# Hybrid encoder layer on one core: the SSD's skip weights in one load of 64-byte rows, sorted by head on GpSimd

## Chip, cores and metric

The kernel runs on one core of a Trainium2 chip. Its time is the time of one execution on the device in microseconds (us); lower is better. A profiled execution gives the rows that are read here. Its span runs from the first to the last instruction.

## The reference, cut to what matters

The program computes one layer of a streaming encoder over 256 tokens of width 1024, in float32: a layer norm, one wide input projection, three mixers (Mamba-2 SSD, RWKV-7, HGRN2), their gated sum, an output projection, a second layer norm, and a mixture of 16 experts with a last layer norm. The part that the change touches is the skip term of the SSD: each of its 16 heads has one weight, `d_skip`, by which the head's input is added to its output.

```
y = y_diag + y_off + xs * d_skip.astype(f32).reshape(SSD_GROUPS, hg)[:, :, None]
```

The RWKV-7 mixer stands beside it in time. Per chunk of 64 tokens it needs the inverse of a triangular matrix for each head, which the kernel gets by forward substitution.

## The kernel before

Activations stand with features on the 128 partitions and tokens along the row. `stream()` (lines 331 to 371) is the inner work of every projection: weights come from memory in pieces of 512 KB into `raw` (line 339, on SyncE's queue, SP), ScalarE (ACT) rounds them to `whi` (line 183), VectorE (DVE) takes the rest `wlo` (line 184), and TensorE (PE) does three products for each tile (lines 366 to 368). There are four buffers of each kind, so a late `wlo` stops TensorE as soon as what is ready is used up.

`mixers()` sets the order. Two halves of the RWKV heads are prepared by `rwkv_part()`, in two calls each. Behind the third call stands the first solve, `rwkv_solve(0)`: GpSimd (POOL) has written the score blocks to DRAM (`ed`, line 536), SyncE's queue loads them again with one system of equations to a partition (`eu`, line 582, four loads of 128 KB in rows of 128 bytes; in the profile both ends are named, as arena<-ed), and VectorE scales them (lines 588, 589) and runs 32 steps of substitution (lines 593, 595). Then comes `ssd_dt_start()`, which issues the loads of the SSD's small vectors on GpSimd's queue behind the last write of `gd` (line 451), and then the fourth `rwkv_part()`. The second solve follows later, from 175 us.

In `ssd_dt_start()` the tile `hp` takes `ssd_dt_bias` and `ssd_a_log` (line 942), each broadcast to 128 partitions as rows of 16 floats, 64 bytes. The tile `dsk` takes the skip weights (line 944) in the order in which the SSD uses them: partitions 0 to 63 hold the even heads, partitions 64 to 127 the odd ones, 8 floats to a partition. The source steps by two floats, so every float is a piece of 4 bytes. `dsk` is read from 449.7 us on (line 1079).

The order of the instructions on each engine is worked out when the program is built, by a planner that goes through the program with its own costs and priorities. Each engine then runs its own list in that order and waits where an operand is not there.

Of the kernel before, what the change touches and what calls it, by code (L numbers as in the profile page):

```python
# [7 lines left out]
F32 = mybir.dt.float32  # L8
# [79 lines left out]
def dram(t, offset, ap):  # L88
    return bass.AP(tensor=t.tensor, offset=t.offset + offset, ap=ap)
# [50 lines left out]
class Kern:  # L140
# [794 lines left out]
    def ssd_dt_start(self):  # L935

        nc, A = self.nc, self.A
        hp = self.hp16 = self.c1.tile([128, 2, 16], F32, name="hp16")
        self.dsk = self.c1.tile([128, 8], F32, name="dsk")
        with self.tc.issue_after(self.later_dma.ins):  # L940
            for i, nm in enumerate(("ssd_dt_bias", "ssd_a_log")):
                nc.gpsimd.dma_start(hp[:, i, :], dram(A[nm], 0, [[0, 128], [1, 16]]))
            for h in range(2):
                nc.gpsimd.dma_start(self.dsk[h * 64:h * 64 + 64, :], dram(A["ssd_d"], h, [[0, 64], [2, 8]]))
        self.sdt = self.c1.tile([128, 5, 16], F32, name="sdT")
        ex = self.dtx = self.c1.tile([128, 2, 16], F32, name="dtx")
        dt = self.sdt[:, 0:2, :]
        ps = self.feat(COL_DT, ncol=16)[:16, 0, :]
        xr = self.rwt.tile([128, L], F32, name="sq")[:16]
        nc.scalar.activation(xr, ps, AF.Copy)  # L950
        ps = self.pmm.tile([128, 2, 16], F32, name="mm")
        for t in range(2):
            nc.tensor.transpose(ps[:, t, :], xr[:, t * 128:(t + 1) * 128], self.ident[:16, :16])
        nc.vector.tensor_tensor(dt, ps, hp[:, 0:1, :].to_broadcast([128, 2, 16]), op=OP.add)
        nc.vector.scalar_tensor_tensor(ex, dt, -1.0, dt, op0=OP.mult, op1=OP.min)
        nc.scalar.activation(hp[:, 1, :], hp[:, 1, :], AF.Exp)
        return nc.scalar.activation(ex, ex, AF.Exp)
# [773 lines left out]
```

## Time and profile before

| | us |
|---|---|
| three runs, median (lowest to highest) | 830.51 (830.09 to 830.99) |
| the profiled execution, its own time | 829.69 |
| its span, first to last instruction | 827.9 |
| TensorE busy in it | 784.8 (95%) |
| VectorE busy in it | 510.1 (62%) |

The profiled execution is 0.82 us under the median; 1.79 us of its time lie outside the span. An engine's busy share is a mean over all stages, so the rows of a stage count for a change in that stage.

### The profile page before, as it was taken

The page shows a single profiled execution, that of the slowest core. Times are in us where ns is not written, and L with a number is a line of the kernel's source. Part 1 is how long each engine was busy: PE and PEld are TensorE (multiplying, and loading weights), DVE is VectorE, ACT ScalarE, POOL GpSimd, SP SyncE. Part 2 cuts the span into 40 slices and gives each one's busy share as a digit, 9 for nine tenths or more (in the row PEclk, how much of TensorE's full clock was granted, in tenths as well). Part 3 has the DMA queues.
Part 4 walks back from the last instruction along what each step waited for, and adds up shares of the span by engine and source line. Part 5 has one row for each costly group of instructions (what it writes and reads, how often), then busy time and mean ns, then how long its engine had stood idle before and what let it go on. Part 6 is the DMA issues. An engine that isn't in the chain of part 4 may idle for free. (4 is left out here: it accounts for less than half of the span.)

```text
span 827.9 us, 16484 instructions
## 1 busy us (share of the span) xinstructions
PE 784.8 (95%) x6354; PEld 604.5 (73%) x6354; DVE 510.1 (62%) x1150; ACT 369.7 (45%) x824; POOL 134.7 (16%) x204
## 2 busy tenths in 40 slices
PE   7999969999999999999998999999999999999991
PEld 5898859988898899898797999999444434443440
DVE  6897669999997555567579887785611111111136
ACT  3755445574645555645477755453412121211111
POOL 3364614450102001102002111000000000001201
PEclk9999969999999999999899999999999999999996
DMA  7544564575445455366179568985999999999941
GB/s 229 177 118 114 50 161 119 140 180 155 107 132 148 128 155 153 103 203 193 38 237 299 178 205 283 349 271 161 390 386 386 387 387 386 387 386 386 386 179 54
DMA packets 146526, 183.93 MB, mean 222 GB/s; under 512 B 25609, under 2 KB 94472, under 8 KB 146440
## 3 DMA queue, kind: packets, MB, share of 16 engines
q1 hardware_dynamic: 142888, 176.91, 65.3%
q0 software_dynamic: 1504, 3.20, 2.2%
q10 hardware_dynamic: 2048, 2.70, 1.0%
q8 instruction: 52, 0.85, 0.4%
q14 instruction: 34, 0.28, 0.1%
HBM read 180.12 MB, written 2.65 MB: 221 GB/s over the span
## 5 line engine op out<-in xcount | busy, mean ns | idle before, releaser
L183 ACT ACTIVATE whi<-raw 128x512 fp32r<-128x512 f32 x268 | 165.5, 623 | 162.9 <-PE st L367 126.3
L184 DVE TENSOR_TENSOR wlo<-raw,whi 128x512 fp32r<-128x512 f32 x268 | 189.1, 715 | 77.3 <-ACT whi L183 64.2
L368 PE MATMUL st<-hhi,wlo 128*128 128x256 f32 (+1 forms) x744 | 212.0, 293 | 9.0 <-DVE wlo L184 8.8
L366 PE MATMUL st<-hhi,whi 128*128 128x256 f32 (+1 forms) x744 | 210.0, 290 | 2.2 <-ACT arena L784 1.4
L367 PE MATMUL st<-hlo,whi 128*128 128x256 f32 (+1 forms) x744 | 208.4, 288 | 0.0
L368 PEld LDWEIGHTS st<-hhi,wlo 128*128 128x128 f32 (+1 forms) x744 | 140.3, 192 | 16.6 <-DVE wlo L184 10.8
L366 PEld LDWEIGHTS st<-hhi,whi 128*128 128x128 f32 (+1 forms) x744 | 140.5, 192 | 7.1 <-issue 2.6
L367 PEld LDWEIGHTS st<-hlo,whi 128*128 128x128 f32 (+1 forms) x744 | 140.3, 192 | 3.1 <-issue 1.6
L1445 PE MATMUL b<-arena,xg 128*64 128x512 f32 x288 | 78.8, 596 | 0.0
L367 PE MATMUL st<-ylo,whi 128*128 128x256 f32 x192 | 53.8, 288 | 1.5 <-DVE ylo L184 1.5
L366 PE MATMUL st<-yhi,whi 128*128 128x256 f32 x192 | 53.9, 287 | 0.0
L368 PE MATMUL st<-yhi,wlo 128*128 128x256 f32 x192 | 53.1, 287 | 0.4 <-DVE wlo L184 0.2
L1445 PEld LDWEIGHTS b<-arena,xg 128*64 128x64 f32 x288 | 23.9, 137 | 38.0 <-issue 34.5
L1515 DVE SCALAR_TENSOR_TENSOR elo<-b,egs,ehi 128x512 fp32r<-128x512 f32 x15 | 11.3, 750 | 60.7 <-ACT ehi L1514 60.7
L1495 PE MATMUL b<-arena,ehT 128*64 128x512 f32 x144 | 43.0, 596 | 0.0
L367 PEld LDWEIGHTS st<-ylo,whi 128*128 128x128 f32 x192 | 36.4, 192 | 2.1 <-DVE ylo L184 1.7
L368 PEld LDWEIGHTS st<-yhi,wlo 128*128 128x128 f32 x192 | 36.2, 193 | 1.0 <-DVE wlo L184 0.8
L366 PEld LDWEIGHTS st<-yhi,whi 128*128 128x128 f32 x192 | 36.5, 192 | 0.3 <-ACT yhi L183 0.2
L1360 POOL TENSOR_TENSOR arena<-arena 128x512 f32<-128x512 bf16 x4 | 4.5, 1158 | 197.2 <-PE b L1445 197.2
L1484 ACT ACTIVATE ehT<-b 128x256 f32<-128x256 f32 x16 | 6.2, 389 | 67.7 <-PE b L1483 67.7
L1476 DVE SCALAR_TENSOR_TENSOR ehi<-ehi,b 128x256 f32<-128x256 f32 x16 | 6.0, 418 | 47.2 <-PE b L1445 47.2
L593 DVE TENSOR_TENSOR arena<-arena 128x1 f32<-128x1 f32 (+15 forms) x64 | 34.0, 531 | 0.8
(448 smaller groups left out, 1431.0 us busy)
## 6 DMA issues: line engine op xcount, KB each, us to landing
raw<-in_w_in_dram SPq DMA_DIRECT2D x102, 512.0 KB, 3.8
arena<-in_exp_w_gate_dram SPq DMA_DIRECT2D x40, 512.0 KB, 10.8
arena<-in_exp_w_down_dram SPq DMA_DIRECT2D x34, 512.0 KB, 10.8
arena<-in_exp_w_up_dram SPq DMA_DIRECT2D x32, 512.0 KB, 10.8
xsl<-in_exp_w_up_dram SPq DMA_DIRECT2D x32, 512.0 KB, 10.8
xsl<-in_exp_w_down_dram SPq DMA_DIRECT2D x20, 512.0 KB, 10.8
xsr<-in_exp_w_gate_dram SPq DMA_DIRECT2D x16, 512.0 KB, 10.8
raw<-in_w_br_rwkv_dram SPq DMA_DIRECT2D x8, 512.0 KB, 4.0
```

The source lines that it names most:

```text
L183: nc.scalar.activation(hi, raw, AF.Copy)
L184: nc.vector.tensor_tensor(lo, raw, hi.bitcast(F32), op=OP.subtract)
L366: nc.tensor.matmul(o, hi[:, kq, fs], xhi[:, k, :], start=st and f == 0, stop=False)
L367: nc.tensor.matmul(o, hi[:, kq, fs], xlo[:, k, :], start=False, stop=False)
L368: nc.tensor.matmul(o, lo[:, kq, fs], xhi[:, k, :], start=False, stop=sp and f == nf - 1)
L593: nc.vector.tensor_tensor(po, tu[:, :n, :t + 1], eu[:, :t + 1, t][:, None, :].to_broadcast([128, n, t + 1]), op=OP.mult)
L1360: nc.gpsimd.tensor_tensor(o, x[1], x[2], op=OP.add)
L1445: nc.tensor.matmul(ps[hs[e]], xg[:, k, hs[e]], W[nm, e, k // 2][:, k % 2, :], start=k == 0, stop=k == KT - 1)
L1476: nc.vector.scalar_tensor_tensor(th[:, c], th[:, c], 0.5, q["pu"][:, c], op0=OP.mult, op1=OP.mult)
L1484: nc.scalar.activation(q["hT"][:, 2 * j:2 * j + 2], tp, AF.Copy)
L1495: nc.tensor.matmul(pd[hs[e], :], q["hT"][:, k, hs[e]], W["exp_w_down", e, (n, k // 2)][:, k % 2, :], start=k == 0, stop=k == 3)
L1515: nc.vector.scalar_tensor_tensor(lo, pd, q["gs"], hi.bitcast(F32), op0=OP.mult, op1=OP.subtract)
```

## The change

The tile `hp` gets a third row, and `ssd_d` is loaded into it as the other two vectors are: one load, 128 partitions, a row of 64 bytes each. Two copies on GpSimd then pick the even heads for partitions 0 to 63 and the odd heads for partitions 64 to 127 into `dsk`. The two loads of 4-byte pieces go. Everything else is as it was.

```
-        hp = self.hp16 = self.c1.tile([128, 2, 16], F32, name="hp16")
+        hp = self.hp16 = self.c1.tile([128, 3, 16], F32, name="hp16")
         self.dsk = self.c1.tile([128, 8], F32, name="dsk")
         with self.tc.issue_after(self.later_dma.ins):
-            for i, nm in enumerate(("ssd_dt_bias", "ssd_a_log")):
+            for i, nm in enumerate(("ssd_dt_bias", "ssd_a_log", "ssd_d")):
                 nc.gpsimd.dma_start(hp[:, i, :], dram(A[nm], 0, [[0, 128], [1, 16]]))
-            for h in range(2):
-                nc.gpsimd.dma_start(self.dsk[h * 64:h * 64 + 64, :], dram(A["ssd_d"], h, [[0, 64], [2, 8]]))
+        for h in range(2):
+            s = slice(64 * h, 64 * h + 64)
+            nc.gpsimd.tensor_copy(self.dsk[s], hp[s, 2, h:16:2])
```

## Rows read from the trace of the kernel before

**Rows 1.** Page: busy time by engine, and TensorE's granted clock in 40 slices

```profile
PE 784.8 (95%) x6354; PEld 604.5 (73%) x6354; DVE 510.1 (62%) x1150; ACT 369.7 (45%) x824; POOL 134.7 (16%) x204
...
PEclk9999969999999999999899999999999999999996
```

**Rows 2.** Windows: stretch, length, busy of PE, PEld, DVE, ACT, POOL, granted clock, DMA

```profile
106.00:108.00 2.00, 0.00 (x0) 0.00 (x0) 0.00 (x0) 0.00 (x0) 0.00 (x0) 0.50 0.90 190
...
116.00:118.00 2.00, 2.00 (x10) 2.00 (x11) 1.97 (x6) 0.84 (x2) 0.54 (x2) 0.50 0.95 280
...
124.00:160.00 36.00, 36.00 (x318) 34.07 (x317) 35.18 (x76) 19.40 (x38) 13.24 (x19) 1.00 0.49 135
...
600.00:640.00 40.00, 40.00 (x264) 17.56 (x262) 6.92 (x17) 7.85 (x19) 0.00 (x0) 1.00 1.05 386
```

**Rows 3.** Timeline of PE: start, length, line; in brackets idle before and releaser

```profile
102.00 0.28 PE L367 MATMUL st<-hlo,whi 128*16 128x256 f32 x1
110.67 0.39 PE L368 MATMUL st<-hhi,wlo 128*16 128x256 f32 x1 [8.39 <-DVE wlo L184]
...
118.28 0.28 PE L368 MATMUL st<-hhi,wlo 128*128 128x256 f32 x1
```

**Rows 4.** Timeline of DVE around the first solve's start

```profile
97.06 0.36 DVE L184 TENSOR_TENSOR wlo<-raw,whi 128x32 fp32r<-128x32 f32 x1
108.52 0.09 DVE L588 MEMSET arena<- 128x32 f32 x1 [11.10 <-DMA arena<-ed]
...
109.78 0.68 DVE L470 TENSOR_TENSOR_SCAN cum<-rst,th 128x256 f32<-128x256 f32 x1
...
110.43 0.18 DVE L184 TENSOR_TENSOR wlo<-raw,whi 128x32 fp32r<-128x32 f32 x1
...
119.14 0.69 DVE L184 TENSOR_TENSOR wlo<-raw,whi 128x512 fp32r<-128x512 f32 x1 [0.78 <-PE st L367]
```

**Rows 5.** DMA issues from 91 to 96 us: count, KB each, median us to landing

```profile
arena<-ed SPq DMA_DIRECT2D x4, 128.0 KB, 13.3
...
dsk<-in_ssd_d_dram POOLq DMA_DIRECT2D x2, 2.0 KB, 10.7
hp<-in_ssd_dt_bias_dram POOLq DMA_DIRECT2D x1, 8.0 KB, 4.2
```

**Rows 6.** Line 582's loads in both solves, fastest, median, slowest

```profile
L582 SPq DMA_DIRECT2D arena<-ed x8: 338/558/2062, 92.3 to 179.4; - x8
...
DMA to landing us min/median/max: 2.7/4.0/14.0
```

**Rows 7.** DMA from 95 to 96 us (first line), then from 96 to 106

```profile
DMA packets 1320, 0.17 MB, mean 170 GB/s; under 512 B 1304, under 2 KB 1320, under 8 KB 1320
...
DMA packets 2012, 0.25 MB, mean 25 GB/s; under 512 B 2012, under 2 KB 2012, under 8 KB 2012
...
q0 software_dynamic: 64, 0.00, 61.4%
```

**Rows 8.** Timeline of SP's queue: issues, last load of line 582 and the next

```profile
95.42 0.59 SPq L582 DMA_DIRECT2D arena<-ed  x1
96.11 9.80 SPq L339 DMA_DIRECT2D raw<-in_w_in_dram  x1
```

**Rows 9.** Timeline of POOL: the small loads and what follows them

```profile
92.33 0.57 POOL L942 DMA_DIRECT2D hp<-in_ssd_a_log_dram  x1
92.89 1.42 POOL L944 DMA_DIRECT2D dsk<-in_ssd_d_dram  x2
95.05 0.47 POOL L466 TENSOR_SCALAR th<-th 128x256 f32<-128x256 f32 x1 [0.74 <-ACT th L465]
...
111.04 0.19 POOL L552 COPY pe<-pc 128x4 f32<-128x4 f32 x1 [12.69 <-ACT pc L474]
```

**Rows 10.** Windows, columns as in rows 2: just behind the small loads' issue

```profile
94.00:96.00 2.00, 2.00 (x18) 2.00 (x18) 1.95 (x5) 1.44 (x4) 1.26 (x3) 1.00 1.05 213
```

**Rows 11.** DMA from 91 to 96 us, GpSimd's queue: packets, MB, share of 16 engines

```profile
q0 software_dynamic: 160, 0.09, 12.5%
```

## Prediction

> **What bounds the kernel now.** The page comes first. TensorE is busy 784.8 us, 95%, VectorE 62%; so a change pays if it takes a hole out of TensorE's work or makes that work quicker. The line of the granted clock shows where to look: 9 in nearly every slice, and 6 in slice six, 103 to 124 us [rows 1]. The windows show what that is: from 106 to 108 us no engine works at all and the clock stands at 0.50, the lower level of 1.2 GHz, and it is still 0.50 from 116 to 118, when TensorE is busy throughout [rows 2]. TensorE's timeline gives the hole: the last matmul starts at 102.00 and ends at 102.28, the next one has been idle for 8.39 us, released by VectorE's `wlo` [rows 3]. So VectorE's timeline is next: it ends a `wlo` at 97.42, then stands 11.10 us in front of line 588 of the first solve, released by a DMA, `arena<-ed`, the loads of `eu`; the `wlo` for which TensorE waits stands behind it in VectorE's list, at 110.43 [rows 4]. This DMA is thus the wait that ends last in this stage, and the one thing to explain is why it is late.
>
> The DMA rows answer that. The four loads of line 582 land 13.3 us after their issue at the median of this stretch, while the fastest of all eight needs 2.7 us and the median of all eight is 4.0 [rows 5, 6]. From 95 to 96 us 1,304 pieces of under 512 bytes went through; in the ten microseconds after that, only 2,012, of which 64 are packets of GpSimd's queue q0, and those 64 took 61.4% of the time of 16 engines [rows 7], 6.1 us of all sixteen. What GpSimd had issued last by then is the pair of `dsk` loads, at 92.89 [rows 9], which themselves take 10.7 us to land for 2 KB each; a load of `hp`, 8 KB in rows of 64 bytes, takes 4.2 [rows 5]. SyncE's queue is caught as well: the issue of the next weight load takes 9.80 us [rows 8]. I read this as: the 1,024 pieces of 4 bytes (128 partitions by 8) hold the DMA engines, and the solve's input waits behind them.
>
> **The change part by part.** *The DMAs.* Two loads of 512 pieces of 4 bytes go, one of 128 pieces of 64 bytes comes. Removed: 6.1 us of all engines. Added: in 91 to 96 us all of q0 (both `hp` loads, the `gd` writes, the start of `dsk`) takes 12.5% of 5 us, 0.6 us [rows 11]; a third load of the kind of `hp` costs 0.3 us at most.
>
> *When the solve's input then lands.* The last of the four loads is issued at 95.42 [rows 8]; with the fastest and the median landing it is there at 98.1 or 99.4 [rows 6]. Counting pieces agrees: the 1,948 (2,012 less 64) that still came after 96 need 1.5 us at the pace of 95 to 96, so not before 97.5 [rows 7]. I take 98.8, where before it was 108.52: VectorE goes on 9.7 us earlier.
>
> *What this does to TensorE.* From line 588 to the end of the awaited `wlo` VectorE needs 2.1 us (108.52 to 110.61) [rows 4]. From 98.8 that is 100.9, and TensorE has matmuls until 102.28: the hole of 8.39 us closes fully, with 1.4 us to spare, and a landing after 100.2 would open it again. Without the hole I see no reason for the lower clock. Between 110.67 and 118.28, 7.6 us, TensorE worked at 0.50 [rows 2, 3]; at full clock that is 3.8 us less at most. TensorE's own bound is 8.39 + 3.8 = 12.2 us.
>
> *What is late next.* VectorE. Its list moves by 9.7 us and it then waits for TensorE once, 0.78 us at 119.14 [rows 4]; since TensorE has gained more, that wait goes: 10.5 us. Behind it, from 124 to 160 us, VectorE is busy 35.18 of 36 us and TensorE 36 of 36 [rows 2], so TensorE can't run ahead of VectorE for long; at most the 0.8 us of idle time left there comes on top. I take 10.5 us, between 9.1 (landing at 99.4, the 0.78 not won) and 12.2.
>
> *GpSimd.* Two issues, 1.42 us, become one of 0.57 [rows 9]. The copies are 64 partitions by 8 floats; nearest below is the copy of 128 by 4, 0.19 us, nearest above the TENSOR_SCALAR of 128 by 256, 0.47. I take 0.2 each, the row that is nearest in size. But the copies wait for the load, and GpSimd's list stands while they do. If the planner puts them right behind the load, `th` (line 466) is behind them: issue at 92.89, landing 4.2 us later at 97.1, copies until 97.5, `th` until 98.0. It is read by VectorE's line 470, which stands 1.26 us behind line 588, so at 100.1. The cover is 2.1 us; from a landing at 99.2 on, each microsecond costs one. If they are put after that group, GpSimd is idle for 12.69 us there [rows 9] and nobody waits. `dsk` itself is wanted only at 450 us, and the extra row of `hp` costs no time.
>
> *The rest of the program.* In the expert stage TensorE is busy 40 of 40 us and the weights run at 386 GB/s [rows 2]; both are near their limit, so a gain reaches the end only if both start earlier. The weight loads stand in the same queue of SyncE behind the `raw` loads and wait for buffers that the earlier stages free, so I let the whole gain through.
>
> *A rule against it.* In 94 to 96 us VectorE was busy 1.95 of 2 us [rows 10], and `hp`'s loads, issued just before, landed in 4.2 us all the same; the `dsk` loads went on dragging while VectorE was idle. The Trainium skill, SBUF — State Buffer, section "SBUF: two separate sides", says that a DMA issued from GpSimd is slow because GpSimd writes its descriptors through a port that VectorE can lock, and that the cure is another issuing queue. By that rule the size of the pieces wouldn't matter, the new load would be as late as a busy VectorE makes it, and the sum would be some 2.4 us smaller; by the rows it stays 10.5.
>
> **The rivals.** *The new load is late and GpSimd stands at the copies* (the rule above is one reason). If its pieces go out only when VectorE falls idle at 97.42, it lands 4.2 us later, at 101.6; copies and `th` end at 102.5, line 470 starts there in place of 109.78: 7.3 us, with the 0.78 8.1, which gives 822.4. If it lands as slowly as `dsk` did, 10.7 us, at 103.6, the same sum gives 6.1 us and 824.4. For it speaks that a wait of this kind is new on GpSimd, against it the 4.2 us of its twin.
>
> *The solve's input is late for another reason* and the change doesn't do what it says: the `hp` loads, or the weight load ahead of it, which stay. Then nothing moves: 830.5. For it: all of these are in flight together. Against it: `hp` takes part in 0.6 us of engine time at most, and the second solve's four loads, without the small vectors beside them, make up the short end of [rows 6].
>
> *Slower: GpSimd's wait takes the place of the wait that goes.* Place: the copies ahead of `th`. Line 470 comes later than today's 109.78 only if the load lands after 108.9, 16.0 us behind its issue; from there each microsecond is lost on VectorE and TensorE, and 0.2% is reached at 17.7 us: 832.2 and up. The slowest landing in this stretch is 14.0 us [rows 6]. It isn't excluded, since neither the load nor the place of the copies is in the trace.
>
> **How the numbers follow.** The sum is made against the profiled execution, 829.69: minus 10.5 is 819.2. That execution is 0.82 under the median, so against the median it is 820.0. My forecast, 818.3 to 821.4 by its own bounds (12.2 and 9.1), gets 0.74; the late load 0.09; no change 0.09; slower 0.08. A difference of about 0.2%, 1.7 us, is what a measurement of this kernel can tell from no change. So faster 0.83, same 0.09, slower 0.08. The range takes in the late load and what the bounds leave out on both sides, since the planner's order may differ by a little everywhere: 817.5 to 826.
>
> **What would show it.** Right: VectorE's idle time ahead of line 588 falls from 11.10 to some 1.4 us, the four loads of line 582 land in 3 to 4 us, the issue of 9.80 us on SyncE's queue is gone, TensorE shows no hole at 102 and a clock of 1.00 through 90 to 130 us, and the expert stage starts some 10 us earlier. The copies' idle time on GpSimd tells how late the new load was. Wrong: `eu` still landing near 108 with no 4-byte pieces about (then they were not the cause); a wait of `cum` for `th` in its place; TensorE gaining 10 us at 120 and losing it to VectorE by 200 or to weights after 580; or another order of VectorE's list, with a new wait elsewhere.

## The result and the profile after

The kernel after takes 818.82 us at the median of four runs (816.11 to 820.18), the kernel before 830.75 beside it on the same chip (four runs): a ratio of 0.9845, with a 95% interval from 0.9823 to 0.9867, or 11.9 us less. The profiled execution of after took 820.18 us, with a span of 818.4, against 829.69 and 827.9. That one execution lies 1.4 us over its median, and that of before 1.1 under its own, so the two traces account for 9.5 us of the 11.9; where the other 2.4 us come from is not shown.

The page of after. Slice six of the granted clock, 6 before [rows 1], is 9; VectorE and TensorE work as long as they did.

```profile
PE 784.8 (96%) x6354; PEld 604.8 (74%) x6354; DVE 511.3 (62%) x1150; ACT 370.3 (45%) x824; POOL 136.7 (17%) x205
...
PEclk9999999999999999999799999999999999999996
```

VectorE's timeline where the first solve starts:

```profile
97.34 0.35 DVE L184 TENSOR_TENSOR wlo<-raw,whi 128x32 fp32r<-128x32 f32 x1
97.61 0.68 DVE L470 TENSOR_TENSOR_SCAN cum<-rst,th 128x256 f32<-128x256 f32 x1
100.05 0.09 DVE L588 MEMSET arena<- 128x32 f32 x1 [1.76 <-DMA arena<-ed]
...
101.50 0.19 DVE L184 TENSOR_TENSOR wlo<-raw,whi 128x32 fp32r<-128x32 f32 x1
```

The wait for the solve's input is 1.76 us in place of 11.10 [rows 4]. Line 588 starts 8.5 us earlier, and the `wlo` that TensorE waited for 8.9. One thing in the order is new: `cum` (line 470), behind line 588 before, now stands ahead of it and fills 0.68 us of the wait. TensorE's order is new as well: the products of line 462, four products behind the hole before, now stand ahead of those four.

The DMA issues from 91 to 96 us, with the KB of each and the median us to landing:

```profile
arena<-ed SPq DMA_DIRECT2D x4, 128.0 KB, 4.7
...
hp<-in_ssd_dt_bias_dram POOLq DMA_DIRECT2D x1, 8.0 KB, 3.9
...
hp<-in_ssd_d_dram POOLq DMA_DIRECT2D x1, 8.0 KB, 4.3
```

And GpSimd's queue from 96 to 106 us, packets, MB and share of 16 engines:

```profile
q0 software_dynamic: 27, 0.01, 1.8%
```

Its 61.4% [rows 7] are gone. The four loads of line 582 land in 4.7 us, not 13.3 [rows 5], and the new load in 4.3, like its twins. The long issue on SyncE's queue [rows 8] is gone: five weight loads are issued between 96.78 and 106.30.

GpSimd's timeline: the new load, and the two copies, which the planner put into the idle stretch behind `th`. They wait for nothing.

```profile
93.16 0.54 POOL L942 DMA_DIRECT2D hp<-in_ssd_d_dram  x1
95.33 0.47 POOL L466 TENSOR_SCALAR th<-th 128x256 f32<-128x256 f32 x1 [1.62 <-ACT th L465]
...
99.07 0.43 POOL L945 COPY dsk<-hp 64x8 f32<-64x8 f32 x2
```

The windows of after, columns as in [rows 2]:

```profile
106.00:108.00 2.00, 2.00 (x18) 1.95 (x17) 1.93 (x7) 1.04 (x3) 0.36 (x2) 1.00 0.93 274
116.00:118.00 2.00, 2.00 (x19) 2.00 (x19) 1.97 (x8) 1.25 (x5) 0.00 (x0) 1.00 0.18 33
124.00:160.00 36.00, 35.23 (x301) 33.35 (x302) 34.86 (x63) 18.23 (x33) 19.27 (x21) 1.00 0.46 128
160.00:170.00 10.00, 9.01 (x71) 8.32 (x70) 10.00 (x15) 8.30 (x14) 6.90 (x5) 0.98 0.82 175
170.00:180.00 10.00, 10.00 (x88) 9.69 (x89) 9.74 (x22) 7.22 (x15) 1.31 (x4) 0.85 0.95 248
```

From 106 to 108 us TensorE is busy throughout, where no engine worked before, and 116 to 118 us run at the upper clock, with 19 matmuls for 10. TensorE has no idle time from 100 to 118 us. The last three lines show where some of the gain is given back, and the timelines say to what. VectorE's:

```profile
135.34 0.18 DVE L586 TENSOR_SCALAR gu<-gu 128x32 f32<-128x32 f32 x1 [0.92 <-DMA gu<-gd]
```

TensorE's:

```profile
153.88 0.39 PE L368 MATMUL st<-hhi,wlo 128*128 128x256 f32 x1 [0.39 <-DVE wlo L184]
155.78 0.38 PE L368 MATMUL st<-hhi,wlo 128*128 128x256 f32 x1 [0.22 <-DVE wlo L184]
...
167.05 0.40 PE L977 MATMUL mm<-dtx,tri 128*128 128x16 f32 x2 [0.99 <-DVE dtx L972]
169.39 0.30 PE L358 MATMUL st<-whi,hhi 128*128 128x256 f32 x1
...
174.59 0.28 PE L360 MATMUL st<-whi,hlo 128*128 128x256 f32 x1
```

Between 169.39 and 174.59 after has a second stretch at the lower clock, which before does not have at this work. TensorE stood idle for 0.99 us ahead of it, at line 977; why the clock fell there is not shown. A window of after, then one of the same work before:

```profile
170.00:172.00 2.00, 2.00 (x11) 2.00 (x11) 1.97 (x5) 2.00 (x6) 0.78 (x3) 0.50 1.03 249
...
180.00:182.00 2.00, 2.00 (x19) 2.00 (x19) 0.79 (x1) 1.09 (x2) 1.98 (x3) 1.00 0.81 130
```

The first and last of these products in TensorE's timeline of before:

```profile
180.18 0.28 PE L358 MATMUL st<-whi,hhi 128*128 128x256 f32 x1
...
183.90 0.28 PE L360 MATMUL st<-whi,hlo 128*128 128x256 f32 x1
```

The products between stand in the same order in both, and TensorE waits for nothing among them: 3.72 us before and 5.20 in after, so this stretch gives back 1.5 us.

Followed from one piece of work to the same piece in the other trace, the gain runs so: 8.5 us at line 588, 8.3 where TensorE goes on past the place of the hole (110.67 to 102.37), 10.6 at the projection behind the scores (115.84 to 105.27), 12.0 at the SSD's transposes (line 953, in after 954; 125.50 to 113.47), 10.8 at line 976 (977; 177.84 to 167.05), 10.2 at line 905 (201.5 to 191.3), 9.6 at the first matmul of the experts' b<-arena,xg (590.4 to 580.8), 9.5 at the end.

### The profile page after: what moved, and what is told of

Its sections match the earlier page's. It is cut to its first block, busy times and chain, and to the rows that moved or that the text cites. A ratio compares the mean times of both kernels' runs of the same rounds, so it can differ in the third digit from the quotient of the medians.

```text
span 818.4 us, 16481 instructions
## 1 busy us (share of the span) xinstructions
PE 784.8 (96%) x6354; PEld 604.8 (74%) x6354; DVE 511.3 (62%) x1150; ACT 370.3 (45%) x824; POOL 136.7 (17%) x205
## 6 DMA issues: line engine op xcount, KB each, us to landing
arena<-in_exp_w_gate_dram SPq DMA_DIRECT2D x40, 512.0 KB, 10.7
arena<-in_exp_w_down_dram SPq DMA_DIRECT2D x34, 512.0 KB, 10.8
arena<-in_exp_w_up_dram SPq DMA_DIRECT2D x32, 512.0 KB, 10.7
xsl<-in_exp_w_up_dram SPq DMA_DIRECT2D x32, 512.0 KB, 10.8
xsl<-in_exp_w_down_dram SPq DMA_DIRECT2D x20, 512.0 KB, 10.8
xsr<-in_exp_w_gate_dram SPq DMA_DIRECT2D x16, 512.0 KB, 10.7
```

## The experiments

Eleven kernels and a second timing of after. All are compared with the kernel before, on the same chip. "Wait" is VectorE's idle time ahead of line 588, "landing" that of line 582's loads issued from 91 to 96 us, "hole" TensorE's idle time ahead of the waiting product; all in us, from one trace each.

| label | added pieces, size, places read | wait | landing | hole | median | ratio (95%) |
|---|---|---|---|---|---|---|
| before | 1,024, 4 bytes, within one 64 bytes | 11.1 | 13.3 | 8.4 | | |
| e2_decoy4 | the same, to no use | 13.3 | 12.7 | 10.2 | 832.09 | 1.0019 (0.9995 to 1.0043) |
| e3_decoy64 | 1,024, 64 bytes, 1 | 11.7 | 11.8 | 8.7 | 830.36 | 0.9977 (0.9946 to 1.0009) |
| e11_one64 | the same, another tensor | 9.9 | 10.3 | 6.8 | 828.15 | 0.9961 (0.994 to 0.9982) |
| e4_actq | as before, ScalarE's queue | 9.6 | 13.5 | 7.5 | 829.85 | 0.9996 (0.997 to 1.0022) |
| e5_half | 512, 4 bytes, within one 64 bytes | 7.6 | 9.9 | 4.9 | 826.53 | 0.9947 (0.9919 to 0.9974) |
| e9_spread4 | 1,024, 4 bytes, 1,024 | 3.6 | 5.6 | 0.4 | 823.07 | 0.9902 (0.9879 to 0.9925) |
| e8_spread64 | 1,024, 64 bytes, 1,024 | 3.4 | 5.5 | 0.3 | 820.86 | 0.9884 (0.9854 to 0.9913) |
| e10_eight64 | 1,024, 64 bytes, 8 | 3.6 | 5.6 | 0.6 | 819.22 | 0.9851 (0.9822 to 0.988) |
| after_again | none | 1.8 | 4.8 | 0 | 818.76 | 0.9849 (0.9822 to 0.9876) |
| e1_later | before, issued at 325.8 us | 0.8 | 4.6 | 0 | 821.44 | 0.9884 (0.9859 to 0.9909) |
| e7_early | after, issued by 3.3 us | 0.6 | 4.2 | 0 | 824.66 | 0.9935 (0.991 to 0.9959) |
| e6_warm | before, matmuls added | 10.7 | 12.7 | 8.1 | 842.35 | 1.0144 (1.0115 to 1.0174) |

**The two old loads brought back, to no use (e2_decoy4).** To the kernel after, behind its own loads:

```diff
+            decoy = self.c1.tile([128, 8], F32, name="decoy")
+            for h in range(2):
+                nc.gpsimd.dma_start(decoy[h * 64:h * 64 + 64, :], dram(A["ssd_d"], h, [[0, 64], [2, 8]]))
```

> The changed kernel, plus the two old loads of 4-byte pieces into a tile that nobody reads. Theory (the 1,024 pieces of 4 bytes hold the DMA engines and the solve's input waits behind them): VectorE stands 8 to 11 us ahead of line 588 again, the last load of line 582 lands at 106 to 109 us, the time is 828 to 832. Rival (the gain comes from the new order of the lists, in which line 470 stands ahead of line 588, not from the DMAs): 817 to 821, since that order stays.

Everything comes back: VectorE's wait, longer than the 8 to 11 us expected, and the whole time. The copies and the new load are still there, so they do not give the gain.

```profile
96.79 0.35 DVE L184 TENSOR_TENSOR wlo<-raw,whi 128x32 fp32r<-128x32 f32 x1
110.47 0.09 DVE L588 MEMSET arena<- 128x32 f32 x1 [13.33 <-DMA arena<-ed]
```

The rival of the order is not settled by this run, since the order did not stay: the planner put `cum` (line 470) behind line 588 again. Two other runs settle it. In e4_actq `cum` stands ahead of line 588, and the wait and the time are there all the same:

```profile
97.05 0.88 DVE L470 TENSOR_TENSOR_SCAN cum<-rst,th 128x256 f32<-128x256 f32 x1
...
108.24 0.09 DVE L588 MEMSET arena<- 128x32 f32 x1 [9.63 <-DMA arena<-ed]
```

In e8_spread64 it stands behind line 588, as here, and the stall is gone:

```profile
100.43 0.09 DVE L588 MEMSET arena<- 128x32 f32 x1 [3.35 <-DMA arena<-ed]
...
102.66 0.68 DVE L470 TENSOR_TENSOR_SCAN cum<-rst,th 128x256 f32<-128x256 f32 x1
```

**As many pieces, sixteen times as large (e3_decoy64).** The inner step becomes zero: all 1,024 pieces are the same 64 bytes.

```diff
+            decoy = self.c1.tile([128, 8, 16], F32, name="decoy")
+            for h in range(2):
+                nc.gpsimd.dma_start(decoy[h * 64:h * 64 + 64], dram(A["ssd_d"], 0, [[0, 64], [0, 8], [1, 16]]))
```

> The changed kernel, plus two loads of 512 pieces each, as many as before, but of 64 bytes, into a tile that nobody reads. Theory (it is the size of 4 bytes that makes a piece dear): 1,024 pieces at no more than 0.3 us for 128 are 2.4 us at most, VectorE waits 2 to 4.5 us ahead of line 588, 819 to 822.5. Rival (it is the number of pieces, each costs the same): 828 to 832, as with the old loads.

830.36 us: with 64-byte pieces the stall is as it was with 4-byte ones. The size of a piece is not what it hangs on. This run alone could not say whether the number of pieces counts, or that all come from one place.

**Half of them (e5_half).**

```diff
+        with self.tc.issue_after(self.later_dma.ins):
+            decoy = self.c1.tile([128, 8], F32, name="decoy")
+            nc.gpsimd.dma_start(decoy[0:64, :], dram(A["ssd_d"], 0, [[0, 64], [2, 8]]))
```

> The changed kernel, plus one of the two loads of 4-byte pieces (512 pieces, 64 partitions) into a tile that nobody reads. Theory (engine time in proportion to the pieces): half of 6.1 us of all engines, VectorE waits 4 to 7 us ahead of line 588, TensorE has a hole of 2 to 5 us, 822 to 827. Rival (one late piece is enough, since a load counts as landed only with its last piece): nearly the whole wait, 827 to 831.

The wait is 7.6 us, a little more than the 4 to 7 expected, between the 1.8 of after and the 13.3 of both loads: 5.9 us for the first 512 pieces, 5.7 for the second, some 11 ns for each piece. The median lies between the two kernels too.

**As many pieces from as many places (e8_spread64, e9_spread4).** The same tile, filled from 1,024 different places of the input projection's weights (`ld` is their row length), with 64 bytes or with 4:

```diff
+            ld = A["w_in"].shape[-1]
-                nc.gpsimd.dma_start(decoy[h * 64:h * 64 + 64], dram(A["ssd_d"], 0, [[0, 64], [0, 8], [1, 16]]))
+                nc.gpsimd.dma_start(decoy[h * 64:h * 64 + 64], dram(A["w_in"], h * 64 * ld, [[ld, 64], [64, 8], [1, 16]]))
```

> As the run with 1,024 additional pieces of 64 bytes, but each piece is read from another place (1,024 places in the projection's weights), into a tile that nobody reads. The run before fell out against the size of 4 bytes. Theory A (every piece on these queues is dear, so their number counts): late solve again, 10 to 13 us of waiting ahead of line 588, 828 to 832. Theory B (1,024 reads of one and the same 64 bytes of memory are served one after the other, and hold everything that stands behind them): no hot place, the pieces go as fast as the 4,096 pieces of line 582, 1 to 4 us of waiting, 818 to 822.

> The changed kernel plus 1,024 pieces of 4 bytes, each read from another place, into a tile that nobody reads. Theory A (number of pieces) and the size of 4 bytes (my prediction's reading): 10 to 13 us of waiting ahead of line 588, 828 to 832. Theory B (reads of one place): 1 to 4 us of waiting, 818 to 822.

The stall is gone in both, though e9_spread4 at 823.07 us lies above the 818 to 822 expected. The DMA issues of e9_spread4 from 91 to 96 us, with 1,024 pieces of 4 bytes in flight:

```profile
arena<-ed SPq DMA_DIRECT2D x4, 128.0 KB, 5.6
decoy<-in_w_in_dram POOLq DMA_DIRECT2D x2, 2.0 KB, 4.7
```

Its VectorE timeline:

```profile
100.70 0.09 DVE L588 MEMSET arena<- 128x32 f32 x1 [3.59 <-DMA arena<-ed]
```

The same two loads in e2_decoy4, as many pieces of the same size but all out of one stretch of 64 bytes, needed 11.4 us to land. So neither 4 bytes nor the number of pieces makes the stall. What the pieces cost by themselves is some 1.8 us of wait (3.6 against 1.8), of which TensorE sees 0.4.

The Trainium skill, DMA: Bandwidth & Descriptors, section "Rules for kernel authors", warns that a last dimension with a step becomes one descriptor per element. The old loads are of that form and so are those of e9_spread4, which added 1.8 us of wait here, not 10; e8_spread64, whose last dimension has no step, added 1.6.

**As many pieces from eight places, 256 bytes apart (e10_eight64).** Each place is read 128 times, as often as one `hp` load reads its row:

```diff
-                nc.gpsimd.dma_start(decoy[h * 64:h * 64 + 64], dram(A["w_in"], h * 64 * ld, [[ld, 64], [64, 8], [1, 16]]))
+                nc.gpsimd.dma_start(decoy[h * 64:h * 64 + 64], dram(A["w_in"], 0, [[0, 64], [64, 8], [1, 16]]))
```

> The changed kernel plus 1,024 pieces of 64 bytes that are read from 8 places, 256 bytes apart, each place 128 times (as often as a load of hp reads its one place), into a tile that nobody reads. Theory B (reads of one place are served one after the other, different places side by side): the 8 places share the work, VectorE waits 3 to 6 us ahead of line 588, 819 to 825. Rival (a broadcast source in itself, or a whole row of memory, is the bottleneck): 10 to 13 us of waiting, 828 to 832.

No stall: the wait is that of 1,024 places, the time that of after. Eight places are enough to spread the reads.

**One place in another tensor (e11_one64).** Up to here the slow loads all read `ssd_d` and the quick ones the weights. From e10_eight64 only the inner step is changed:

```diff
-                nc.gpsimd.dma_start(decoy[h * 64:h * 64 + 64], dram(A["w_in"], 0, [[0, 64], [64, 8], [1, 16]]))
+                nc.gpsimd.dma_start(decoy[h * 64:h * 64 + 64], dram(A["w_in"], 0, [[0, 64], [0, 8], [1, 16]]))
```

> The kernel after, and behind its small loads two more into a tile that nobody reads: 1,024 pieces of 64 bytes, as in the run with eight places, but all from one and the same 64 bytes of the input projection's weights. It differs from that run in the number of places alone (1 for 8), and from the earlier run with one place in the tensor that is read. Theory, many reads of one place are served one after the other, whichever tensor holds it: the time returns to about 830 us, VectorE waits 10 to 13 us at line 588, the loads of line 582 land in 11 to 13 us. Rival, the skip weights' own tensor is slow, where it lies in DRAM, and the number of reads of one place has nothing to do with it: about 819 us as with eight places, a wait of some 3.6 us and landings of 5.6 us.

The stall is back. The trace of e11_one64, by the same two views, DMA issues first:

```profile
arena<-ed SPq DMA_DIRECT2D x4, 128.0 KB, 10.3
decoy<-in_w_in_dram POOLq DMA_DIRECT2D x2, 32.0 KB, 9.7
```

VectorE's timeline:

```profile
107.11 0.09 DVE L588 MEMSET arena<- 128x32 f32 x1 [9.85 <-DMA arena<-ed]
```

Wait and landings are at or just under the lower edge expected, but 6.2 and 4.7 us above those of eight places; the time is 828.15, for 819.22. So it is not the tensor. It is a little less than with `ssd_d` (9.9 against 11.7 us of wait, one trace each), which no run explains.

**The old loads from ScalarE's queue (e4_actq).** In the kernel before:

```diff
-        nc.scalar.activation(ss, gps, AF.Copy)
+        self.later_act = nc.scalar.activation(ss, gps, AF.Copy)
...
+        with self.tc.issue_after(self.later_act.ins):
             for h in range(2):
-                nc.gpsimd.dma_start(self.dsk[h * 64:h * 64 + 64, :], dram(A["ssd_d"], h, [[0, 64], [2, 8]]))
+                nc.scalar.dma_start(self.dsk[h * 64:h * 64 + 64, :], dram(A["ssd_d"], h, [[0, 64], [2, 8]]))
```

> The kernel before, with the two loads of 4-byte pieces issued from ScalarE's queue, just behind line 449, in place of GpSimd's. Theory (the pieces hold the DMA engines, whoever issues them): the loads of line 582 land late again, 8 to 11 us of waiting ahead of line 588, 828 to 833. Rival (GpSimd is slow at writing the descriptors of so many pieces, and that is what drags): the loads land in 5 us or less and the time is 818 to 822.

Nothing is gained (0.9996). ScalarE issues the pair at 90.0 and 90.8 us. The DMA issues from 91 to 96 us:

```profile
arena<-ed SPq DMA_DIRECT2D x2, 128.0 KB, 13.5
gd<-ss POOLq DMA_DIRECT2D x2, 2.0 KB, 9.5
dsk<-in_ssd_d_dram ACTq DMA_DIRECT2D x1, 2.0 KB, 11.8
hp<-in_ssd_dt_bias_dram POOLq DMA_DIRECT2D x1, 8.0 KB, 13.1
```

SyncE's queue:

```profile
92.33 13.60 SPq L582 DMA_DIRECT2D arena<-ed  x4
```

The windows, columns as in [rows 2]:

```profile
91.00:96.00 5.00, 5.00 (x41) 4.54 (x41) 3.91 (x9) 3.09 (x8) 2.85 (x6) 1.00 0.12 14
96.00:100.00 4.00, 4.00 (x35) 3.74 (x34) 2.60 (x5) 2.17 (x6) 2.78 (x6) 1.00 0.05 0
```

What is issued behind the pair by 96 us, on SyncE's queue or GpSimd's, takes 9.5 to 13.8 us to land, while from 96 to 100 us the DMA engines show a share of 0.05 and move next to nothing, and SyncE needs 13.60 us to issue four loads (4.09 in after). The issuing engine is not the cause.

On this queue the pieces can be counted: 1,056 packets from 91 to 106 us, about one for each of the 1,024 pieces. DMA from 96 to 100 us, ScalarE's queue, columns as in [rows 11]:

```profile
q10 hardware_dynamic: 419, 0.00, 4.6%
```

That is a piece every 9.5 ns, and 4.6% of 16 engines is 0.7 of one engine at work on them. The Trainium skill agrees as far as it goes: DMA: Bandwidth & Descriptors, section "Issuing engines are not separate DMA queues", says that loads from ScalarE, SyncE and GpSimd run on the same 16 engines. The cure named by the rule that the prediction weighed (the Trainium skill, SBUF — State Buffer, section "SBUF: two separate sides") does not work here: another issuing queue has the same stall.

**The old loads later (e1_later).** In the kernel before, moved behind the last GpSimd operation of the HGRN mixer's preparation (its line 865, fourth pass), where nobody waits for a DMA:

```diff
-        nc.gpsimd.tensor_tensor(k2, bc, bc[:, :, 63:64].to_broadcast([128, 8, 64]), op=OP.subtract)
+        k2d = nc.gpsimd.tensor_tensor(k2, bc, bc[:, :, 63:64].to_broadcast([128, 8, 64]), op=OP.subtract)
+        if j == 3:
+            with self.tc.issue_after(k2d.ins):
+                for h in range(2):
+                    nc.gpsimd.dma_start(self.dsk[h * 64:h * 64 + 64, :],
+                                        dram(self.A["ssd_d"], h, [[0, 64], [2, 8]]))
...
-            for h in range(2):
-                nc.gpsimd.dma_start(self.dsk[h * 64:h * 64 + 64, :], dram(A["ssd_d"], h, [[0, 64], [2, 8]]))
```

> The kernel before with its two loads of 4-byte pieces issued some 250 us later, behind the last head group of HGRN2 on GpSimd, where no solve waits for a load. All theories of a collision: the loads of line 582 land in 3 to 5 us, the hole at 102 us is gone; at the new place the weight loads are held for some 10 us, which four buffers hide in part: 818 to 824. Rival (the loads cost something wherever they stand, or the gain comes from the load being one): 826 to 831.

821.44 us: most of the gain without any other kind of load. Issued at 325.8 us they still need 10.4 us to land, but from there to 340 us no engine is seen to wait on a DMA. So the slow loads matter because the solve's input is issued within 3 us of them.

**All three small loads at the program's start (e7_early).** In the kernel after, the loop over `hp` is moved ahead of the first layer norm's constants:

```diff
+        hp = self.hp16 = self.c1.tile([128, 3, 16], F32, name="hp16")
+        for i, nm in enumerate(("ssd_dt_bias", "ssd_a_log", "ssd_d")):
+            nc.gpsimd.dma_start(hp[:, i, :], dram(A[nm], 0, [[0, 128], [1, 16]]))
...
-        hp = self.hp16 = self.c1.tile([128, 3, 16], F32, name="hp16")
+        hp = self.hp16
...
-        with self.tc.issue_after(self.later_dma.ins):
-            for i, nm in enumerate(("ssd_dt_bias", "ssd_a_log", "ssd_d")):
-                nc.gpsimd.dma_start(hp[:, i, :], dram(A[nm], 0, [[0, 128], [1, 16]]))
```

> The changed kernel with all three loads of 64-byte rows issued at the start of the program, ahead of the mixers. Theory B: even three loads with 128 reads of one place each hold the solve's input a little (VectorE still waits 1.76 us); without them it waits 0 to 1 us, TensorE has no hole in either, so the time is that of the changed kernel or up to 1 us less: 816.5 to 819.5. Rival: at the start the three loads hold the first inputs and the time is 1 to 4 us more.

VectorE's wait falls to 0.57 us, the least of all, yet the time is 824.66. The loss is far away: the last matmul of line 690 (687 in after) is at 409.5 us and at 409.3 in after, but the first of line 1178 at 557.5 for 553.9. From 430 to 440 us TensorE was busy 7.04 us at a granted clock of 0.66, against 8.10 at 0.83 in after. The planner gave that stage another order. So differences of 2 to 6 us between kernels that have no stall say nothing on the loads, and the runs e1_later, e7_early, e8_spread64, e9_spread4 and after are not ranked against each other.

**TensorE kept busy through the hole (e6_warm).** In the kernel before, nine matmuls on constants were meant to stand in the hole, so that the lower clock behind it could be priced by itself:

```diff
-                            nc.tensor.matmul(o, hi[:, kq, fs], xlo[:, k, :], start=False, stop=False)
...
+                            was = nc.tensor.matmul(o, hi[:, kq, fs], xlo[:, k, :], start=False, stop=False)
+                            if ncol == 16 and k == 6:
+                                with self.tc.issue_after(was.ins):
+                                    was = self.warm(self.pmm.tile([128, 4, 128], F32, name="mm"), 9)
...
```

> The kernel before, with nine matmuls of 512 columns on constants (some 8 us of TensorE's time) put into TensorE's list ahead of the product that waits for wlo. The wait stays, but TensorE is not idle in it. Theory (the lower clock from 104 to 118 us comes from the idle time, and costs up to 3.8 us): the clock stays at 1.00, VectorE still waits some 11 us ahead of line 588, 826.5 to 829. Rival (the clock costs nothing, since VectorE sets the pace behind the hole): 829.5 to 832.

A miss. TensorE's timeline still has its hole, ahead of other work that the planner put first and that waits for VectorE too, and the nine ran behind it, from 123 us, for some 7 us; the kernel became 11 us longer.

```profile
110.84 1.12 PE L523 MATMUL mm<-ident,vp 64*64 64x64 f32 x16 [8.08 <-DVE arena L600]
```

This run says nothing on the price of the clock.

**After, timed again (after_again).**

> The changed kernel once more, beside the others on one chip: 816 to 820.5.

818.76 us, ratio 0.9849 (0.9822 to 0.9876): the gain stands.

## Why the prediction was right, and where it was not

The forecast was 820.0 us, and 818.82 came: its likeliest case. That the size is so near is in part luck, since two terms were off and against each other ("What is late next" and "The rest"). The chain, solve's input late, then VectorE, then TensorE, then the clock, is the one that e2_decoy4 switched on again and that e5_half showed at half strength.

**The cause as read.** The step that failed is the reading that "the 1,024 pieces of 4 bytes (128 partitions by 8) hold the DMA engines". They do hold them, but not for being small or for being 1,024: e9_spread4 has both and no stall, and e3_decoy64 and e11_one64 have 64 bytes a piece and the whole of it. What counts is that all 1,024 are read from the same 64 bytes of DRAM. The change cures this not by its longer rows but because only 128 reads go to that place, once for each partition. The share of 61.4% [rows 7] was read as time in which the engines worked on those pieces, which can't be told from it; in e4_actq such a pair blocked everything while all queues together show a share of 0.05. The forecast came out all the same, since any reading in which the pair is at fault takes the same wait away.

**Landing.** 98.8 was taken; line 588 starts at 100.05, 8.5 us earlier and not 9.7, since the loads took 4.7 us to land, more than the 2.7 and 4.0 of [rows 6] from which the value was taken. Three `hp` loads still cost something: without them the wait is 0.57 (e7_early, with its other order).

**TensorE.** The hole closed, with 0.6 us to spare where 1.4 was said: the awaited `wlo` ends at 101.69, ahead of the 102.28 at which TensorE ran out [rows 3]. The later landing cost more than that, but `cum` was done ahead of line 588, so that from there to the end of the `wlo` VectorE needs 1.6 us for 2.1. In after TensorE also has line 462's products to do first and takes up the awaited product only at 102.99.

**The clock.** Up to 3.8 us were allowed, and 3.3 came. The work that TensorE did before from 110.67 to 118.28 [rows 3], at 0.50, takes it from 102.37 to 106.69 in after, at 1.00: the same products, though line 462 comes first now, 7.61 us and 4.32.

```profile
102.37 0.70 PE L462 MATMUL ch<-xwa,wa 64*128 64x256 f32 x2
...
106.69 0.59 PE L507 MATMUL mm<-sq,blk 128*128 128x256 f32 x2
```

With the 8.3 us of the hole that is 11.6. It is read from the two traces; the experiment that was to isolate it failed. The second stretch at the lower clock, of after alone, gives a price with the order unchanged: 1.5 us for the work of 3.72.

**What is late next.** VectorE was to hold the gain at 10.5 us, and it did not: at 125 us TensorE had gained 12.0, close to its own bound of 12.2, and VectorE 11.5 at line 954 (955; 126.43 to 114.89). The 0.78 us wait of [rows 4] is gone, and so are three shorter ones of VectorE between 123 and 128 us, 0.7 us together, which the sum had only as an amount on top; what the rest came from, in an order that is new, is not shown. The loss comes later: 0.92 us on VectorE at 135.34, for `gu`, for which nothing waits in the trace of before, 0.61 us on TensorE at 153 to 156, 0.99 at line 977 for 0.75 before, and the lower clock behind it.

**GpSimd.** The copies took 0.43 us, where two of 0.2 were said, and stand in the idle stretch: free, by the second of the two cases named.

**The rest.** The whole gain was let through, and from the 12.0 us at 125 us 10.2 are left at 200, 9.6 ahead of the experts and 9.5 at the end of the span: only the expert stage lets it through as assumed. The sum's 10.5 stands against 9.5 between the two traces and 11.9 between the medians.

**The rivals.** The late new load: it landed in 4.3 us. Another cause for the late input: the `hp` loads and the weight load stayed, and the stall went. GpSimd's wait: there is none.

## What to carry to other kernels

Before a small tensor is spread over partitions by a load with a step of zero, count how often one and the same place of DRAM is read: 128 reads were cheap here, 1,024 held up the transfers beside them for some 10 us. Read a row once for each partition and pick the elements on an idle engine, or issue the load where nobody waits for a DMA. And test the cause that a change is said to remove with a load that nobody uses: it separates size, number and place of the pieces in a few runs.

## What the runs showed of the hardware

Many reads of one place are served slowly, and what is issued behind them waits, whatever queue either came from. Against the 1.8 us of after, 512 reads added 5.9 us to VectorE's wait and 1,024 added 7.9 to 11.6, some 8 to 12 ns for each; 1,024 reads of eight places 256 bytes apart, 128 of each, or of 1,024 places added 1.6 to 1.9. It is so for 4 and for 64 bytes, for two tensors, and for loads issued from GpSimd and from ScalarE. SyncE's issues drag with it: 9.80 us [rows 8] for one load before, 13.60 for four in e4_actq. That the reads are served one after the other is argued, from the price for each and from the 0.7 of one engine at work in e4_actq; which part of the path does so, and how far apart two places must lie below 256 bytes, was not tried.
